# Index loads of a max-unpooling kernel issued from GpSimd, with 32-bit words cast to bytes on the way

## Chip, cores, metric

One core of one Trainium2 chip. The metric is device time of one execution in microseconds (us). The kernel before takes 74.55 us (median of 3 runs, 74.49 to 74.62). A profile covers one execution; its span, from the first to the last recorded instruction, is some 1.7 us shorter than the time.

## The reference

```python
x:       (16, 64, 32, 32) float32
indices: (16, 64, 32, 32), values 0..3     # kernel_size = 2
output = zeros((16, 64, 64, 64))
for b, c, i, j:
    idx = indices[b, c, i, j]
    output[b, c, 2*i + idx // 2, 2*j + idx % 2] = x[b, c, i, j]
```

Each input value goes to one of the four places of its 2 x 2 field; the other three stay zero. Nothing is summed. The indices reach the chip as 64-bit integers, so 1,048,576 of them are 8.39 MB; x is 4.19 MB and the output 16.78 MB.

## The kernel before

128 partitions hold eight images of 32 x 32 each. x comes in one load from SP, the indices in two loads of half the images from ACT, seen as pairs of 32-bit words of which VectorE reads the low one. Four output tiles follow, each filled by four VectorE instructions (one for each place of the field) and stored by SP.

```python
x_t = ld.tile([P, T * H * W], mybir.dt.float32, tag="x")
nc.sync.dma_start(out=x_t[:], in_=x_v)                       # 4.19 MB
idx_ts = []
for g in range(2):
    idx_t = ld.tile([P, T * H * W], mybir.dt.int32, tag="idx", bufs=2)
    nc.scalar.dma_start(out=idx_t[:], in_=idx_v32[g])        # 4.19 MB each
    idx_ts.append(idx_t)
# ... idx_c: the low word of each pair, a step of two words ...
for s in range(n_st):                                        # n_st = 4
    out_t = st.tile([P, MS * 4 * H * W], mybir.dt.float32)   # 3 buffers
    # ...
    for pidx in range(4):
        # ... hoff, woff = pidx // 2, pidx % 2: the place in the field ...
        nc.vector.scalar_tensor_tensor(                      # (idx == pidx) * x
            out=o_c[:, :, :, hoff, :, woff], in0=idxs, scalar=pidx, in1=xs,
            op0=mybir.AluOpType.is_equal, op1=mybir.AluOpType.mult)
    nc.sync.dma_start(out=out_v[s], in_=out_t[:])            # 4.19 MB each
```

## Time and profile before

| | before |
|---|---|
| span | 72.8 us |
| 16 DMA engines busy | 94.5% of the span |
| VectorE busy | 49% of the span |
| first VectorE instruction | 22.78 us |
| first store issued | 31.70 us |
| bytes moved | 29.36 MB |

The prediction below shows the lines that this comes from. Digits in the rows of 40 slices are tenths of a slice, here of 1.82 us. A queue row gives packets, MB written by them, and the time of its packets as a share of 16 engines' span. "us to landing" runs from the issue of a transfer to its last byte.

### The profile page before, as it was taken

How to read it: one execution, taken by the hardware profiler on the slowest of the kernel's cores; microseconds unless marked ns; L12 is line 12 of the kernel's file. 1: busy time of each engine (PE TensorE's matmuls, PEld its weight loads, DVE VectorE, ACT ScalarE, POOL GpSimd, SP SyncE). 2: the span in 40 equal slices, each digit the busy share in tenths (PEclk: the TensorE clock that was granted, in tenths of full speed). 3: DMA queues.
4: the chain of work that ended last, by engine and by line, in shares of the span. 5: the costliest groups of instructions: out<-in, count | busy, mean ns of one | idle time of the engine just before them, and what ended most of it. 6: DMA issues, size and time to landing. Idle time of an engine off the chain costs nothing.

```text
span 72.8 us, 70 instructions
## 1 busy us (share of the span) xinstructions
DVE 35.3 (49%) x16; POOL 0.2 (0%) x4
## 2 busy tenths in 40 slices
DVE  0000000000004999999999999999999900000000
POOL 1000000000000000000000000000000000000000
DMA  3798989898989899966969696969797979798980
GB/s 108 234 522 360 504 360 504 360 504 360 504 360 504 378 486 414 450 288 288 576 288 576 288 576 288 576 288 558 306 540 324 558 306 522 342 486 378 486 378 0
DMA packets 1008, 29.36 MB, mean 403 GB/s; under 512 B 112, under 2 KB 112, under 8 KB 112
## 3 DMA queue, kind: packets, MB, share of 16 engines
q1 hardware_dynamic: 720, 20.97, 67.8%
q10 hardware_dynamic: 288, 8.39, 26.7%
HBM read 12.58 MB, written 16.78 MB: 403 GB/s over the span
## 4 chain that ended last, share of the span: by engine, by line
DVE 43%; DMA 30%; DVEq 6%; issue 0%
DVE out_t L65 43%; DMA idx_t<-in_indices_dram 30%; DVEq L105 6%
## 5 line engine op out<-in xcount | busy, mean ns | idle before, releaser
L65 DVE SCALAR_TENSOR_TENSOR out_t<-idx_t,x_t 128x2048 f32<-128x2048 int32 x16 | 35.3, 2284 | 22.8 <-DMA idx_t<-in_indices_dram 22.8
L91 POOL MEMSET const-bfloat16-1.0<- 128x1 bf16 x1 | 0.1, 101 | 0.0
L91 POOL MEMSET const-uint8-127<- 128x1 uint8 x1 | 0.1, 101 | 0.0
L91 POOL MEMSET const-float32-0.0<- 128x1 f32 x1 | 0.1, 98 | 0.2 <-issue 0.2
L91 POOL MEMSET const-float32-1.0<- 128x1 f32 x1 | 0.1, 98 | 0.0
## 6 DMA issues: line engine op xcount, KB each, us to landing
out_dram<-out_t SPq DMA_DIRECT2D x4, 4096.0 KB, 12.5
idx_t<-in_indices_dram ACTq DMA_DIRECT2D x2, 4096.0 KB, 26.6
x_t<-in_x_dram SPq DMA_DIRECT2D x1, 4096.0 KB, 21.9
```

The lines of the kernel that those rows point to most:

```text
L65: nc.vector.scalar_tensor_tensor(out=o_c[:, :, :, hoff, :, woff], in0=idxs, scalar=pidx, in1=xs, op0=mybir.AluOpType.is_equal, op1=mybir.A ...
L91: nc = _bacc.Bacc("TRN2", target_bir_lowering=False, num_devices=1)
L105: with _tile.TileContext(nc) as tc:
```

## The change

The intent: the kernel needs one byte of each index but lets eight land in SBUF. A load issued from GpSimd can convert on the way, so that 4.19 MB of words are written as 1.05 MB of bytes. Where the written bytes set the time of a transfer, that would save 6.3 MB of traffic. The cap of 8192 bytes cuts each row into four pieces of 2048 words.

```diff
     for g in range(2):
-        idx_t = ld.tile([P, T * H * W], mybir.dt.int32, tag="idx", bufs=2)
-        nc.scalar.dma_start(out=idx_t[:], in_=idx_v32[g])
+        idx_t = ld.tile([P, T * H * W], mybir.dt.uint8, tag="idx", bufs=2)
+        nc.gpsimd.dma_start(out=idx_t[:], in_=idx_v32[g], max_dma_last_dim=8192)
         idx_ts.append(idx_t)
```

A comment line in the launch part also went; nothing else changed.

## The prediction

> **What bounds the kernel now.** I read the page from the top: busy shares, the 40 slices, the DMA queues. Then the chain of waits, and last the waits and the order in time.
>
> ```profile
> span 72.8 us, 70 instructions
> DVE 35.3 (49%) x16; POOL 0.2 (0%) x4
> DVE  0000000000004999999999999999999900000000
> DMA  3798989898989899966969696969797979798980
> q1 hardware_dynamic: 720, 20.97, 67.8%
> q10 hardware_dynamic: 288, 8.39, 26.7%
> HBM read 12.58 MB, written 16.78 MB: 403 GB/s over the span
> ```
>
> VectorE works 49% of the span and is idle in its first and last third. The DMA row is near full from the second slice to the last but one. The queue rows add up to 67.8 + 26.7 = 94.5% of 16 engines' span, which is 68.8 us of 72.8. So the 16 DMA engines are the bound: 29.36 MB in 68.8 us of engine time is 427 GB/s. Of it, q10 is the index loads (8.39 MB, 26.7% of 72.8 = 19.4 us, 432 GB/s, so 9.7 us for each of the two), and q1 is x (4.19 MB, a fifth of its 49.4 us, about 9.8 us) and the four stores (16.78 MB, about 39.5 us).
>
> The chain of waits, in order of time, and the waits:
>
> ```profile
> 0.73 22.03 DMA idx_t<-in_indices_dram
> 22.75 0.02 issue
> 22.78 20.10 DVE out_t L65 x10
> ...
> DVE out_t L65 <- DMA idx_t<-in_indices_dram: 22.8, 1, 22.8
> ```
>
> VectorE waits once, for the first index load, then never again. x shares the engines with that load: 8.39 MB at 430 GB/s is 19.5 us, plus about 2 us until the first data packet, gives the observed landing (21.9 us for x). The rest follows from these rows:
>
> ```profile
> L65 DVE SCALAR_TENSOR_TENSOR out_t<-idx_t,x_t 128x2048 f32<-128x2048 int32 x16 | 35.3, 2284 | 22.8 <-DMA idx_t<-in_indices_dram 22.8
> out_dram<-out_t SPq DMA_DIRECT2D x4, 4096.0 KB, 12.5
> idx_t<-in_indices_dram ACTq DMA_DIRECT2D x2, 4096.0 KB, 26.6
> x_t<-in_x_dram SPq DMA_DIRECT2D x1, 4096.0 KB, 21.9
> ```
>
> A quarter of the output is four VectorE instructions of 2.28 us, about 9.0 us; the first store is issued at 31.7 us (order in time), just as the second index load, alone on the engines from about 22 us, has run its 9.7 us. Then four stores of 9.8 us follow without a gap, since a quarter costs VectorE less than its store costs the engines: 31.7 + 4 x 9.8 = 70.9 us, plus about 1.5 us for the last landing and the end of the program, is the span. The profile can be written as one sum: about 2 us start + 9.8 (x) + 9.7 + 9.7 (indices) + 39.2 (stores) + 2 us end and small gaps = 72.4 us. Nearly every microsecond is time of the DMA engines; only what changes that sum, or opens a gap in it, moves the end.
>
> **What the Trainium skill says.**
> (1) "DMA: Bandwidth & Descriptors", section "SWDGE vs HWDGE vs iDMA": a cast in flight can be issued from GpSimd only; there a pair of its cores computes a read and a write descriptor per piece in software; the same 16 engines move the data, and each takes turns between the queues. The profile before has only hardware-generated queues (q1, q10), so it shows nothing of the software path. That two queues take turns agrees: x and the first index load, issued together, land within a microsecond of each other.
> (2) The same page, "Where 436 GB/s comes from": 16 ports of 32 bytes at 850 MHz, 435 GB/s. The 432 GB/s of q10 agree: these loads already run at that ceiling.
> (3) "VectorE: DVE Perf Modes", section "What auto-detection actually checks": the double rate of a two-input instruction needs every tensor to be 16-bit with step 1. Here x and out stay fp32, so bytes in place of words do not qualify. The 2284 ns for 2048 elements are 1.07 cycles of 0.96 GHz per element, the single rate.
> (4) "SBUF — State Buffer", section "Who interferes with whom": a VectorE instruction with two SBUF inputs contends with GpSimd reading SBUF, not with GpSimd only writing it. Descriptor writing should then not be held up. No row of the profile before tests it.
>
> No page gives the rate of a casting transfer from words to bytes. That is the gap in this prediction.
>
> **The change part by part.**
>
> (a) Bytes. Each index load still reads 4.19 MB from HBM (the low and the high 32-bit word of every index), and now writes 1.05 MB to SBUF in place of 4.19. The read traffic of the kernel is the same: 12.58 MB from HBM plus 16.78 MB out of SBUF. If an engine is occupied by the wider side of a transfer, a load costs the same 9.7 us and the sum does not move: 0 us. I take this as the main case, because 432 GB/s is both what these loads read and what they write, so nothing in the profile says that the write side is the limit.
>
> (b) Pieces. Today a load is 128 pieces of 32 KB; q10 has 288 packets, of which 32 are the small ones that signal the end, so 19.4 us x 16 / 256 = 1.21 us each. The new cap of 8192 bytes makes 4 pieces of each row: 64 per engine for both loads in place of 16. 32 KB at 27.2 GB/s (the page's 435 / 16) would be 1.205 us, so a piece costs perhaps 8 ns extra. Estimate: 48 more pieces x 8 ns = 0.4 us; with three times that for software descriptors, 1.2 us.
>
> (c) Issue. ACT's two issues (0.88 us together in the order in time) go; GpSimd must compute 512 reads and 512 writes per load before data flows. x, still issued at 0.73 us by SP, alone occupies the engines for 9.8 us. So as long as the first batch is ready before about 12 us, the engines never idle, and x and the first index load together still end at about 22 us, whichever of the two goes first. The second batch is computed during the transfer of the first. Cost on the path: 0, up to 1 us if the engines start these queues in a staggered way.
>
> (d) VectorE. 16 instructions at the single rate with a step of 2 bytes instead of 8: 16 x 2.28 us unchanged. It is not the bound: 0 us.
>
> (e) Memory. The index tiles shrink from 64 to 16 KB per partition, but the pool of output tiles stays at three, so nothing new may start earlier.
>
> Sum of the main case: 0 + 0.4 to 1.2 + 0 to 1 + 0 = 0.4 to 2.2 us, of which part disappears in the small gap between the end of the second index load and the first store. I take +0.9 us: 74.55 + 0.9 = 75.4 us, and 75.6 with a little weight for the tail of rival 1.
>
> **The rivals.**
>
> Rival 1, the converter is slower than the wire. If it takes words at half the rate, the two loads cost 38.8 us of the engines in place of 19.4. First VectorE instruction at about 2 + 9.8 + 19.4 = 31 us, second load ending among the stores, span about 72.8 + 19.4 = 92 us, time about 94 us. A buffer that is filled and emptied in turn (a quarter more per piece, since the output is a quarter of the input) would give +4.9 us: 79.4 us. A quarter of the rate gives +58 us, 133 us. For it: the profile shows no casting transfer, so nothing rules it out[...]. Against: the loads need only 432 / 16 = 27 GB/s per engine, 8 words per 850 MHz cycle.
>
> Rival 2, the write side is what counts. Then a load costs 9.7 / 4 = 2.4 us; x and the first index load are in at about 2 + 9.8 + 2.4 = 14.2 us, the second before 17 us, the first store goes out at 14.2 + 9.0 = 23.2 us, four stores end at about 62.4, plus 1.9 for the end gives a span of 64.3 us and a time near 66 us. VectorE, done at 14.2 + 36.5 = 51 us, does not hold it. For it: the skill calls the SBUF ports the limit. Against: one engine also reads at 27 GB/s when it stores.
>
> Rival 3, the turns are unfair. If the index queue took many pieces per turn, both index loads would pass before x; VectorE would start near 32 us, the engines would idle some 9 us until the first store, about 83 us. The opposite unfairness, x first, costs nothing, as in (c).
>
> **Range and chances.** Main case, 74.2 to 77 us: a little under 0.6, and perhaps a quarter of it over 76.04 us (2%). Rival 1 about 0.3, spread over 78 to 133 us with most at or below 94; rival 3 about 0.05; rival 2 about 0.08 (below 73.06 us). So faster 0.08, same 0.46, slower 0.46. Predicted 75.6 us; low 73.8, cutting off rival 2; high 94, half the rate.
>
> **What would show it.** Step (a): the software queue's share of 16 engines times the span should be near 19.4 us; 38 us or more is rival 1, under 8 us is rival 2. Step (b): a packet of 8 KB taking about 0.31 us. Step (c): the first VectorE instruction at 22 to 24 us and a DMA row full from the second slice; zeros there would be slow descriptors, and a late landing of x would be rival 3. Step (d): 2284 ns, with uint8 in the shape. The prediction is wrong if the first VectorE instruction starts after 25 us or before 20 us, or if the stores, which nothing here touches, no longer follow one another at 9.8 us.

## More of the kernel before

One more view was read after the prediction: a stretch in which the second index load has the engines to itself. The columns are the stretch and its length, busy time and instruction count of VectorE and GpSimd, the TensorE clock, the share of the DMA engines, and GB/s of written bytes.

```profile
core 0: us, DVE busy (x) POOL busy (x), PEclk, DMA share, GB/s
24.00:30.00 6.00, 6.00 (x4) 0.00 (x0) 1.00 1.00 431
```

Index words move at 431 GB/s, in pieces of 32 KB (a piece is one packet record of the trace). One engine starts a new piece every 1209.4 ns here. That spacing is the yardstick of the experiments. The records do not name the engine, so the start of each piece is compared with that of the sixteenth piece after it, and the mean is taken over the same stretch, 24 to 30 us.

## The result

The changed kernel is correct and takes 74.71 us (median of 4 runs, 74.51 to 74.82), against 74.57 us for the kernel before in the same rounds. The ratio is 1.0011, with a 95% interval of 0.9992 to 1.003. Ratios here and below are the mean time of a kernel's runs over that of the kernel before in the same rounds, so they are not quite the ratio of the medians. A gain of 0.1% or a loss of 0.3% would both fit.

The page of the changed kernel, the lines that answer to those shown of before:

```profile
span 73.0 us, 70 instructions
DVE  0000000000004999999999999999999900000000
DMA  3899899799999999996979797979797979797960
q1 hardware_dynamic: 720, 20.97, 68.0%
q0 software_dynamic: 1056, 2.10, 28.4%
HBM read 12.58 MB, written 16.78 MB: 402 GB/s over the span
```

The index loads have moved to a software queue, and they write 2.10 MB in place of 8.39. But the DMA row is as full as it was, VectorE's row is the same digit for digit, and HBM reads the same 12.58 MB.

The chain of waits and the waits:

```profile
1.23 21.70 DMA idx_t<-in_indices_dram
...
22.95 20.11 DVE out_t L65 x10
...
DVE out_t L65 <- DMA idx_t<-in_indices_dram: 23.0, 1, 23.0
```

The chain has the same links: the first index load lands at 22.93 us, not earlier, and VectorE follows 0.17 us later than before. The groups of instructions and the transfers:

```profile
L65 DVE SCALAR_TENSOR_TENSOR out_t<-idx_t,x_t 128x2048 f32<-128x2048 uint8 x16 | 35.3, 2287 | 23.0 <-DMA idx_t<-in_indices_dram 23.0
L44 POOL DMA_DIRECT2D idx_t<-in_indices_dram x2 | 1.6, 810 | 0.8 <-PEq L105 0.8
...
out_dram<-out_t SPq DMA_DIRECT2D x4, 4096.0 KB, 12.5
x_t<-in_x_dram SPq DMA_DIRECT2D x1, 4096.0 KB, 14.3
idx_t<-in_indices_dram POOLq DMA_DIRECT2D x2, 1024.0 KB, 26.1
```

VectorE is no faster with bytes (2287 ns against 2284). x lands after 14.3 us in place of 21.9: its 32 KB pieces now take turns with pieces of 8 KB, so x goes first and the index load makes up for it. As VectorE needs both, nothing is won. The stores land after 12.5 us, as before. The last line gives the written size, 1024 KB; what the engines were occupied for is told by the stretch that was read before:

```profile
24.00:30.00 6.00, 6.00 (x4) 0.00 (x0) 1.00 1.07 108
```

108 GB/s of bytes are 432 GB/s of words read. The load reads as fast as it did without the cast, to within 1%, and the written three quarters that are gone gave no time back. The share of 1.07 shows a trap: the packets of the casting queue are recorded as 324 ns long, but an engine starts one every 304.7 ns; the records overlap. So the 28.4% of q0 overstates its time. The spacing gives 64 x 304.7 = 19.50 us per engine for both loads, against 16 x 1209.4 = 19.35 us before.

### The profile page after: what moved, and what is told of

It reads as the page before. It is cut to its first block, busy times and chain, and to the rows that moved or that the text cites. A ratio compares the mean times of both kernels' runs of the same rounds, so it can differ in the third digit from the quotient of the medians. Undisturbed runs are those within 1.5% of the kernel's fastest.

```text
span 73.0 us, 70 instructions
## 1 busy us (share of the span) xinstructions
DVE 35.3 (48%) x16; POOL 1.8 (2%) x6
## 3 DMA queue, kind: packets, MB, share of 16 engines
q0 software_dynamic: 1056, 2.10, 28.4%
HBM read 12.58 MB, written 16.78 MB: 402 GB/s over the span
## 4 chain that ended last, share of the span: by engine, by line
DVE 43%; DMA 30%; DVEq 6%; issue 1%; PEldq 0%
DVE out_t L65 43%; DMA idx_t<-in_indices_dram 30%; DVEq L105 6%; PEldq L105 0%
## 5 line engine op out<-in xcount | busy, mean ns | idle before, releaser
L65 DVE SCALAR_TENSOR_TENSOR out_t<-idx_t,x_t 128x2048 f32<-128x2048 uint8 x16 | 35.3, 2287 | 23.0 <-DMA idx_t<-in_indices_dram 23.0
L44 POOL DMA_DIRECT2D idx_t<-in_indices_dram x2 | 1.6, 810 | 0.8 <-PEq L105 0.8
## 6 DMA issues: line engine op xcount, KB each, us to landing
out_dram<-out_t SPq DMA_DIRECT2D x4, 4096.0 KB, 12.5
x_t<-in_x_dram SPq DMA_DIRECT2D x1, 4096.0 KB, 14.3
```

The source lines that it names most:

```text
L44: nc.gpsimd.dma_start(out=idx_t[:], in_=idx_v32[g], max_dma_last_dim=8192)
L65: nc.vector.scalar_tensor_tensor(out=o_c[:, :, :, hoff, :, woff], in0=idxs, scalar=pidx, in1=xs, op0=mybir.AluOpType.is_equal, op1=mybir.A ...
```

## The experiments

The theory (A): an engine is occupied by the wider side of a casting transfer, so the cast is free and useless here; pieces lose some ns each; and a late start of the software queue is hidden behind x. The rivals: the conversion costs something that something else gives back; the late start is paid; or the read side sets the time, not the wider one. Four runs tested pieces and conversion. hard_8k and n8_before are edits of the kernel before; all other runs are edits of the changed kernel.

### whole_rows: the cast without the cap

```diff
-        nc.gpsimd.dma_start(out=idx_t[:], in_=idx_v32[g], max_dma_last_dim=8192)
+        nc.gpsimd.dma_start(out=idx_t[:], in_=idx_v32[g])
```

> The changed kernel without the cap on a piece: a whole index row of 8192 words in one piece. Theory A (an engine is occupied by the wider side, and pieces follow one another with about 2 ns lost at each, as the spacing of 305 ns in the changed kernel says): 16 pieces per engine in place of 64, about 1.21 us apart, software queue near 27% of the span, 74.6 us, at most 0.2 us from the changed kernel. Theory B (the converter fills a buffer and empties it, hidden so far by the short pieces): a quarter more per long piece, about +4.8 us, 79 us. If it is right, the cap was never needed.

Measured: correct, 74.53 us, ratio 0.9991 (0.9979 to 1.0003). The stretch from 24 to 30 us:

```profile
24.00:30.00 6.00, 6.00 (x4) 0.00 (x0) 1.00 1.02 109
```

A piece of 32 KB read and 8 KB written starts every 1208.2 ns, 1 ns under the plain copy. Theory B, a buffer filled and emptied in turn, is out. The cap was not needed for a right result or for speed.

### soft_nocast: GpSimd's queue, words written as words

```diff
-        idx_t = ld.tile([P, T * H * W], mybir.dt.uint8, tag="idx", bufs=2)
+        idx_t = ld.tile([P, T * H * W], mybir.dt.int32, tag="idx", bufs=2)
```

> The changed kernel without the cast: 32-bit words still issued from GpSimd in 8 KB pieces, written as they are. Theory A (neither the conversion nor the software descriptors cost time of the engines): 74.6 us, pieces about 303 to 305 ns apart, same first VectorE instruction within 0.2 us. Theory C (the conversion costs some of it and the narrower write gives some back, so that two effects cancel in the changed kernel): the time moves by over 0.5 us when the cast is taken away, in either direction.

Measured: correct, 74.88 us, ratio 1.0047 (1.0031 to 1.0063).

```profile
24.00:30.00 6.00, 6.00 (x4) 0.00 (x0) 1.00 1.02 423
```

The pieces are 310.6 ns apart, more than theory A gave (303 to 305), and the time is about 0.35 us over the kernel before, and about 0.27 us over the changed kernel by the two ratios. The move is below the 0.5 us that theory C asked for. But a trace of C is there: with the narrow write a piece costs 6 ns less (304.7) than with the full one, 0.4 us over 64 pieces. Why is open.

### hard_8k: ACT's queue, no cast, 8 KB pieces

```diff
-        nc.scalar.dma_start(out=idx_t[:], in_=idx_v32[g])
+        nc.scalar.dma_start(out=idx_t[:], in_=idx_v32[g], max_dma_last_dim=8192)
```

> The kernel before, ACT queue and no cast, with its index rows cut into pieces of 8 KB. Theory A: 48 more pieces per engine at 2 ns, 0.1 us, time 74.6 to 74.7 us. The record's step (b) (8 ns or more per extra piece): +0.4 us, 75.0 us, less what the gap before the first store takes up. One thing it may also show: 8 KB turns of the index queue against 32 KB turns of x let x land at about 15 us in place of 22.6.

Measured: correct, 74.75 us, ratio 1.0021 (1.0009 to 1.0033), and x landed after 14.6 us.

```profile
24.00:30.00 6.00, 6.00 (x4) 0.00 (x0) 1.00 1.01 421
```

The spacing is 310.5 ns, the same as from GpSimd to within 0.1 ns. So the software queue as such costs an engine nothing; the length of the pieces does. The loss is 310.5 - 1209.4 / 4 = 8.2 ns for each 8 KB, the record's 8 ns and not theory A's 2, or 64 x 8.2 = 0.52 us for both loads. The last index byte comes 0.40 us later than before (32.55 us against 32.15), yet the first store is issued only 0.07 us later (31.77 us): the part that falls on the second load vanishes in the gap ahead of the first store.

### cast_1k: the cast in 1 KB pieces

```diff
-        nc.gpsimd.dma_start(out=idx_t[:], in_=idx_v32[g], max_dma_last_dim=8192)
+        nc.gpsimd.dma_start(out=idx_t[:], in_=idx_v32[g], max_dma_last_dim=1024)
```

> The changed kernel with pieces of 1 KB (256 words read, 256 bytes written): 512 pieces per engine in place of 64, so that a cost per piece shows. Theory A (about 2 ns lost per piece): 512 x 2.3 = 1.2 us over the pure 19.3, against 0.15 now, so about +1.0 us at most, 74.7 to 75.7 us. The record's step (b) with 8 to 24 ns per piece: +3.6 to +11 us, 78 to 86 us. A third possibility is that computing 4096 read and 4096 write descriptors per load on GpSimd takes longer than the 9.8 us of x and leaves the engines empty: then zeros in the DMA row before 22 us.

Measured: correct, 75.67 us, ratio 1.0146 (1.0133 to 1.0159).

```profile
24.00:30.00 6.00, 6.00 (x3) 0.00 (x0) 1.00 1.46 99
```

```profile
L44 POOL DMA_DIRECT2D idx_t<-in_indices_dram x2 | 3.5, 1744 | 0.8 <-PEq L105 0.8
```

A piece takes 41.2 ns, 3.4 ns over a 32nd of 1209.4. Over 512 pieces that is 1.75 us; half of it falls on the first load, and VectorE starts 0.97 us later than before (23.75 us). The time is 1.1 us longer, just outside theory A's "at most" in the trace (2.3 ns was a little low) and inside its range in the time; the record's 8 to 24 ns are far off. Eight times the pieces took GpSimd twice as long (1744 ns per load against 810), and left no hole.

### late_4 and late_12: GpSimd held up ahead of the loads

```diff
     idx_ts = []
+    wait_t = ld.tile([P, 4096], mybir.dt.float32, tag="wait")
+    for _ in range(1):           # range(4) in late_12
+        nc.gpsimd.memset(wait_t[:], 0.0)
     for g in range(2):
```

> The changed kernel with one GpSimd fill of a 128 x 4096 fp32 scratch tile (estimate: 3 to 4 us) ahead of the two index loads. It tests step (c): x alone occupies the engines for 9.8 us, so a late start of the index loads is free up to about 11.8 us. Theory A: first index piece some 3 to 4 us later than in the changed kernel (6.15 us there), x lands earlier, first VectorE instruction still at 22.9 us, time 74.7 us. Rival (the queues being served together is what fills the engines, so any delay is paid): 77 to 79 us.

> The same with four such fills (estimate: 12 to 16 us). Theory A: the engines have run through x at about 11.8 us and then idle until the first index piece; the time grows by the start of the first index piece minus 11.8 us, less up to 0.8 us: with a first piece at 15 to 19 us, 77 to 82 us. First VectorE instruction at first piece plus 9.8 us.

Measured: late_4 74.69 us, ratio 1.0015 (0.9999 to 1.003); late_12 74.73 us, ratio 1.0015 (1.0001 to 1.0029). In late_4 the fill took 3.51 us, GpSimd began to issue the loads at 4.19 us in place of 1.23, the first index piece began at 8.8 us in place of 6.15, and VectorE at 22.73 us. So an issue 3.0 us later cost nothing. late_12 is a miss of the experiment: the scheduler put two of its four fills behind the loads and one between them, so the first load was no later than in late_4. It says nothing about a long delay, and was done again.

### late_7 and late_12b: one fill, longer

```diff
     idx_ts = []
+    wait_t = ld.tile([P, 8192], mybir.dt.float32, tag="wait")   # 14336 in late_12b
+    nc.gpsimd.memset(wait_t[:], 0.0)
```

> Second try at step (c), since the scheduler spread the four fills of the run late_12 among and behind the loads. The changed kernel with one fill of 128 x 8192 fp32 ahead of both loads (7.0 us, by the 3.51 us measured for half of it). In three runs the first index piece came 4.6 to 4.9 us after GpSimd began the issue, so it is due at about 12.3 us, just as x (alone from 2.0 us, 8 pieces of 1.213 us) ends at about 11.8 us. Theory A: still free, or up to 0.6 us: 74.7 to 75.3 us. If part of the 4.6 us is only standing behind pieces of x, it starts sooner and costs nothing.

> The same with one fill of 128 x 14336 fp32 (12.3 us): GpSimd begins the issue at about 13.0 us, after x has ended. Theory A: the engines stand idle from about 11.8 us until the first index piece, and the whole of that gap is paid: first piece at 14.3 us (if a software start takes 1.3 us without x in the way) to 17.6 us (if the 4.6 us are its own), first VectorE instruction 9.8 us plus 0.3 us later, time 77.2 to 80.5 us. Rival (the late start is taken up somewhere, since VectorE has slack against the stores): under 76 us.

Measured: late_7 74.7 us, ratio 1.0005 (0.9989 to 1.0021); late_12b 77.33 us, ratio 1.0358 (1.0341 to 1.0375). In order of time, late_7:

```profile
0.73 6.92 POOL L43 MEMSET wait_t<- 128x8192 f32 x1 [0.29 <-POOLq L93]
...
7.60 1.62 POOL L46 DMA_DIRECT2D idx_t<-in_indices_dram  x2
22.91 35.33 DVE L67 SCALAR_TENSOR_TENSOR out_t<-idx_t,x_t 128x2048 f32<-128x2048 uint8 x16 [22.91 <-DMA idx_t<-in_indices_dram]
```

and late_12b, with its engines just after x:

```profile
0.74 12.04 POOL L43 MEMSET wait_t<- 128x14336 f32 x1 [0.29 <-POOLq L93]
...
12.72 1.62 POOL L46 DMA_DIRECT2D idx_t<-in_indices_dram  x2
25.47 35.33 DVE L67 SCALAR_TENSOR_TENSOR out_t<-idx_t,x_t 128x2048 f32<-128x2048 uint8 x16 [25.47 <-DMA idx_t<-in_indices_dram]
```

```profile
12.00:14.00 2.00, 0.00 (x0) 2.00 (x3) 1.00 0.00 0
```

In late_7 GpSimd begins 6.4 us later than in the changed kernel and VectorE starts at the same time (22.91 us against 22.95). In late_12b the last pieces of x end at 12.35 to 12.82 us, the first index piece starts at 14.55, the engines take up nothing between 12 and 14 us, and VectorE starts 2.5 us late; the time grows by 2.7 us. So the cover is the transfer of x, as step (c) said, and what lies beyond it is paid in full. The rival, that VectorE's slack takes it up, is out. In late_12b the first piece came 1.83 us after GpSimd began to issue; beside x it was 4.9 us in the changed kernel, 4.6 in late_4 and 4.7 in late_7. So some 3 us go with x being on the engines. That the index pieces stood behind pieces of x is the likely reading; no run shows it directly.

### widen_store: the opposite cast

```diff
-        out_t = st.tile([P, MS * 4 * H * W], mybir.dt.float32)
+        out_t = st.tile([P, MS * 4 * H * W], mybir.dt.bfloat16)
...
-        nc.sync.dma_start(out=out_v[s], in_=out_t[:])
+        nc.gpsimd.dma_start(out=out_v[s], in_=out_t[:], max_dma_last_dim=8192)
```

> The opposite cast, on the transfers that fill most of the span: output tiles in bf16, stored from GpSimd with a cast to fp32 (read 2 bytes, write 4). The result is rounded, wrong on purpose at about 0.4%. Theory A (the wider side of a casting transfer sets its time): a store still takes 9.8 us of the engines, and the software start puts the first store off by 1 to 4 us: 75.5 to 79 us, VectorE as before. Rival (the read side sets it, which the cast to bytes could not tell apart): a store takes about 4.9 us, VectorE becomes the bound, its last instruction at about 59 us, time near 67 us.

Measured: 76.08 us, ratio 1.0187 (1.0171 to 1.0203); the rounded output passed the comparison. A stretch filled by stores alone, and the two groups:

```profile
36.00:70.00 34.00, 23.56 (x11) 2.24 (x3) 1.00 1.12 430
```

```profile
L65 DVE SCALAR_TENSOR_TENSOR out_t<-idx_t,x_t 128x2048 bf16<-128x2048 uint8 x16 | 36.7, 2399 | 22.9 <-DMA idx_t<-in_indices_dram 22.9
L74 POOL DMA_DIRECT2D out_dram<-out_t x4 | 3.0, 747 | 54.7 <-DVE out_t L65 54.7
```

430 GB/s of fp32 are written while 215 GB/s of bf16 are read; within a store, a piece of 8 KB written starts every 303.5 ns. So it is not the read side that counts, which the narrowing cast could not tell, but the wider one. One rival stays untested: in both casts the wider side is also the side in HBM. No run has the wider side in SBUF (a widening load or a narrowing store), so "the wider side" and "the HBM side" are not told apart here. The 1.4 us lost over the kernel before are a VectorE instruction of 2399 ns in place of 2284 (4 of them, 0.5 us, ahead of the first store; why bf16 output is slower here stays open), a software start of 1.55 us where SP needs 1.08 (first store issued at 32.45 us, data at 34.0), and, not separated further, the rest.

### n8_before and n8_cast: eight output tiles of half the size

```diff
-    n_st = 4
+    n_st = 8
-    st = ctx.enter_context(tc.tile_pool(name="st", bufs=3))
+    st = ctx.enter_context(tc.tile_pool(name="st", bufs=6))
-        idxs = idx_c[s // 2][:, MS * (s % 2) : MS * (s % 2) + MS]
+        idxs = idx_c[s // 4][:, MS * (s % 4) : MS * (s % 4) + MS]
```

n8_cast is the same edit on whole_rows.

> The kernel before with eight output tiles of 2 MB in place of four of 4 MB (six buffers of half the size). Theory A says that only time of the engines counts, and that the last loss beside start and end is the hole of about 1.0 us between the end of the second index load and the first store. With half tiles the first store is ready about 4.6 us earlier, while index bytes are still coming in, so the hole goes: 73.4 to 73.7 us, first store issued at about 27.6 us, last VectorE instruction near 62 us at the latest. Rival: half the store size costs as much in landings, or loads and stores at once slow each other: 74.5 us or more.

> The same with the casting index loads from GpSimd, a whole row to a piece. Theory A: the cast stays free and the hole goes as in the run beside it: 73.3 to 73.7 us, within 0.2 us of it. If the two differ by over 0.5 us, the cast or the software queue costs something when stores run beside it.

Measured: both correct; n8_before 75.0 us, ratio 1.0059 (1.0046 to 1.0071); n8_cast 75.33 us, ratio 1.01 (1.0086 to 1.0114). Theory A's step on the hole fell. n8_before, around the first store, which was issued at 27.37 us:

```profile
28.00:31.00 3.00, 3.00 (x4) 0.00 (x0) 1.00 1.31 404
31.00:33.00 2.00, 2.00 (x3) 0.00 (x0) 1.00 0.29 123
33.00:36.00 3.00, 3.00 (x4) 0.00 (x0) 1.00 1.02 437
```

The hole is still there, although the store was waiting in its queue for 4 us. In the packet records the last two pieces of the second index load on nearly every engine stretch from 1.21 us to as much as 1.8 and 2.2 us, the load ends at 33.3 us in place of 32.15, and the first store packet starts at 32.7 us, as late as before. So an earlier store did not buy an earlier start of stores.

In the kernel before, the hole is the start of the store itself. The store was issued at 31.70 us, the index pieces ended between 31.49 and 32.15 us, and the first store packet came at 32.78 us, 1.08 us after the issue; in every run with four tiles stored from SP this start took 1.07 to 1.09 us. Turning from loads to stores need not leave a hole: in cast_1k the store was issued at 32.68 us, its packets started at 33.77, and index pieces ran until 34.26. Two us of the kernel before (first line) and of cast_1k (second line; records that overlap or run on past the stretch make a share over 1):

```profile
31.00:33.00 2.00, 2.00 (x2) 0.00 (x0) 1.00 0.61 262
33.00:35.00 2.00, 2.00 (x2) 0.00 (x0) 1.00 1.62 536
```

So the stretched pieces of n8_before are another loss than the hole that theory A wanted to close. Why they stretch is open, and so is why n8_cast lost 0.3 us more than n8_before. No version tried beats the kernel before by more than the noise; whole_rows ties with it.

## Why the prediction was right or wrong

The direction (no gain) and what bounds the kernel (the DMA engines) were right; the sum was too large: it said 75.6 us, +1.05, and the measured difference is +0.14 with an interval that includes zero. What failed is its two allowances, steps (b) and (c), of which it took +0.9 us: the runs show 0.15 us for (b) and 0 for (c).

- **Step (a), bytes: right.** A load costs the wider side (or the HBM side, as said above; here they are the same). 432 GB/s of words read in the cast, and 430 GB/s of fp32 written in widen_store, rule out the read side and the write side as such. Rival 2 is out.
- **Step (b), pieces: the term that was mis-sized.** The record put 0.4 to 1.2 us in the sum. A casting piece of 8 KB loses 304.7 - 1209.4 / 4 = 2.3 ns against the plain long copy, so 64 of them lose 0.15 us. The 8 ns had come from comparing a packet's time with a page's ceiling; that it is just what an uncast piece loses (8.2 ns in soft_nocast and hard_8k) is luck, and the cast loses less. The allowance of three times that for software descriptors has no counterpart at all, since both queues show 310.5 ns to within 0.1. The half that falls on the second load has the gap before the first store to disappear in.
- **Step (c), issue: right in mechanism, its allowance of up to 1 us mis-sized.** The engines never idled, and late_7 shows 6.4 us more delay costing nothing; late_12b shows the cover ending where x ends. The term is 0.
- **Steps (d) and (e): right.** 2287 ns against 2284, and no store began earlier.
- **The weight for rival 1 (+0.2 us in the point, 0.3 of the chances): not needed.** There is no slow converter: whole_rows has 1208.2 ns for a piece of 8192 words. This was the record's one real gap, and nothing in the profile before could close it.
- **Rival 3** did not come: turns went piece by piece, in favour of x, the harmless direction.
- **The record's own test for (a)**, the share of the software queue times the span, reads 28.4% of 73.0 = 20.7 us, more than the true 19.5, because casting packets overlap in the records. Spacing or GB/s of the wider side in a stretch with one queue is the better test.
- **The skill's point (4).** "SBUF — State Buffer", "Who interferes with whom", agrees: GpSimd's issue of a store took 746 to 748 ns in widen_store, three times with VectorE at work and once after its end, against 747 to 874 ns for the index loads of the changed kernel with VectorE idle.
- **Two loose readings in the working** moved nothing. The 21.9 us of x count from its issue at 0.73 us, so x landed at 22.6 us, 1 us after the 21.5 us of that sum. And the stores could not follow from 31.7 us: the first packet came 1.08 us after the issue, so that the last store packet ended at 71.9 us and not at 70.9.

VectorE's start 0.17 us later is more than the 0.08 us that half of 0.15 accounts for; the first VectorE instruction of whole_rows came 0.23 us earlier than in the kernel before, so differences of this size between single profiles are not explained here.

## What to carry to other kernels

On a kernel bound by DMA engines, count the wider side of each transfer where that side is in HBM, as it was in both casts here: narrowing the landing side of this load shortened neither the load nor the kernel, though it freed SBUF and did no harm. A later or slower start of one queue is free as long as another queue has transfers to fill the engines until then; work out how long that cover is, here the 9.8 us of x. When an estimate has a mechanism but no measured size, measure it by the spacing in a short run (hard_8k and soft_nocast were such runs), and do not add allowances on top of it.

## What the Trainium skill lacked or had wrong

- "DMA: Bandwidth & Descriptors" has no rate for a casting transfer. Measured: words to bytes 432 GB/s of words read (8 KB read every 304.7 ns per engine, 32 KB every 1208.2 ns); bf16 to fp32 430 GB/s written. The wider side, which was the HBM side in both, moved at the plain copy's rate.
- The same page, "SDMA does more than copy", gives 2048 as the greatest element count of the collective-compute unit (CCE), and does not say whether a cast goes through it. For a pure cast the runs show no such limit: whole_rows converted 8192 words in a piece, correctly and at full rate.
- The same page, "Latency and other measured facts", gives about 1 us to the first byte for the software path and 0.6 us for the hardware one, and does not say from which point it counts. From the start of the issue to the first packet the runs show 1.83 us (late_12b) and 1.55 us (widen_store) in software, 1.08 us for the first store from SP in the kernel before, and 4.9 us in software beside another queue's 32 KB pieces.
- No page has it that the record times of casting packets overlap (324 ns long, 304.7 ns apart), so that a queue's share of the engines reads too high (20.7 us for 19.5). Uncast pieces of 8 KB do not overlap (309 ns long, 310.6 ns apart).
- No page has it that the last pieces of a load stretch where stores wait behind it: in n8_before, with the first store issued 4.3 us earlier, from 1.21 us to as much as 2.2 us, and the first store packet came at 32.7 us, as late as before.
